# Shifted places for the stationary operands of gate and up, and a ring of eight places

## The chip, the cores and the metric

The kernel runs on one core of a Trainium2 chip. The metric is device time in microseconds (us), from the start to the end of one execution. Of the engines, TensorE (PE in the profile, its weight loads PEld) multiplies, VectorE (DVE), ScalarE (ACT) and GpSimd (POOL) do elementwise work, and SyncE's queue (SP) issues most DMAs.

## What is computed

The reference is one decoder layer. The change touches the first half of its last part, the products of a normalised activation with two weight matrices:

```python
fn = rms_norm(h, norm_ffn[l])                  # 1024 x 1024
g = fn @ ffn_w_gate[l]                         # 1024 x 2816
g_conv = ffn_conv_b[l] + sum(cw[i] * g_pad[:, i:i + s] for i in range(CONV_W))
h = h + (jax.nn.silu(g_conv) * (fn @ ffn_w_up[l])) @ ffn_w_down[l]
```

Ahead of it stand a gated linear attention, a causal attention, their output projection and a cross-attention over 256 memory tokens; none of them is touched.

## The kernel before, in words

All products keep float32 accuracy by splitting both operands into a high and a low part (`split`, L77: ScalarE writes the high part at L66, VectorE subtracts it and writes the low part at L69) and by multiplying three times: low by high, high by low, high by high.

Gate and up are computed in 11 pairs `j` of column blocks; a pair covers 256 columns of `ffn_w_gate` (`m_` 0, called g below) and the same of `ffn_w_up` (`m_` 1, called u). Each half is a 2 x 2 block product done with seven products in place of eight: P1, P6, P5, P7, P2, P3, P4, in this order (`ORDER`, L1328). Pairs 0 and 1 take P1 and P2 from matmuls made earlier, so that 146 products are left. Below, 2uP3 is product P3 of the up half of pair 2.

A product (`product`, L1214) is 12 matmuls, each with a 128 x 128 stationary operand from the weights and 512 moving columns from the activations (tiles `obP3` to `obP7`, `fh`, `fl`). They stand at L1220, L1221 and L1222.

The stationary operands of a product are made by `prep` (L1332). The raw weights of a half pair lie in a tile `rw` (1 MB, loaded by SyncE's queue in `raw_load`, L1231). For P1, P2 and P4 the source is a part of `rw`; for the others it is a sum in the tile `ss`, which GpSimd makes (VectorE for 0g). There is one `ss`, so the sums of a half pair start when the split of the P3 before it, the last reader, is done. The first three of the four GpSimd operations have to be over before P6 can be split. The split's result goes into a place `op`, 4096 bytes a partition: the high part, then the low part, each of four 128 x 128 blocks. Places are taken in turn from a list (`RING`). Seven are there at first; from 2uP1 on, two more join, whose room is held until then by the tiles `x1`. A place can be written again when TensorE has done the product that read it. `prep` runs 6 products ahead of `run` in pairs 0 and 1 and 8 ahead later (L1414).

After its products, `run` (L1368) adds PSUM banks into `GU` on VectorE. Two of these additions gate TensorE: P7 adds into the bank of P6, so it has to wait until `GU <- p, P` has read P6; P3 adds into the bank of P5, so it waits until `GU <- GU, P` has read P5. The tile `p` is ScalarE's copy of P1. Between them stand the convolution and silu of the gate (`conv`, two steps on VectorE at L72, two activations on ScalarE).

No order is written out by hand: a scheduler in the language's tile layer puts each engine's instructions into a queue by program order, priorities and its own costs, and each queue then runs strictly in that order.

Of the kernel before, what the change touches and what calls it, by code (L numbers as in the profile page):

```python
# [10 lines left out]
F32 = mybir.dt.float32  # L11
F32R = mybir.dt.float32r
# [6 lines left out]
P = 128  # L19
# [14 lines left out]
def build(tc, a, out):  # L34
# [6 lines left out]
    @contextmanager  # L41
    def pri(off):
        tc.cur_priority -= off
        yield
        tc.cur_priority += off
# [11 lines left out]
    def pool(name, side=None):  # L57
        return tc.tile_pool(name=name, bufs=1, reuse_waits="tile", **({"side": side} if side else {}))

    def k16(shape, dt, name):  # L60
        return big.tile(shape, dt, name=name, tag="k16", bufs=8)
# [3 lines left out]
    def act(o, i, f, **kw):  # L65
        nc.scalar.activation(out=o, in_=i, func=f, **kw)  # L66

    def tt(o, x, y, op, eng=None):
        (eng or nc.vector).tensor_tensor(out=o, in0=x, in1=y, op=op)  # L69
# [7 lines left out]
    def split(hi, lo, src, gain=None):  # L77
        if gain is None:
            act(hi, src, AF.Copy)
            tt(lo, src, f32(hi), ALU.subtract)  # L80
        else:
            act(hi, src, AF.Copy, scale=gain)
            stt(lo, src, gain, f32(hi), ALU.mult, ALU.subtract)
# [182 lines left out]
    def pj(n, name="pj"):  # L266
        pjn[0] += 1
        return pjc[pjn[0] % pjn[1]].tile([P, 512], F32, name=name, tag="pj", bufs=1)[:, 0:n]
# [11 lines left out]
    def proj(W, n, t):  # L280
        o = pj(n)
        mm3(o, [(xblk(xh, t)[:, k], xblk(xl, t)[:, k], W[k][0], W[k][1]) for k in range(KD)])
        return o
# [53 lines left out]
    for t in range(NB):  # L337
# [5 lines left out]
        o = proj(W, 256, t)  # L343
# [14 lines left out]
    for t in range(NB):  # L358
        o = proj(W, 304, t)
# [5 lines left out]
        x1, x2 = kpe[:, 0:16], kpe[:, 16:32]  # L365
# [34 lines left out]
    for mh in range(2):  # L400
        W = load_chunk((pBc, pAc)[mh], a["w_in"], C_Q + 256 * mh, 256, KD, f"wq{mh}", R_NM, wb=8)
        for m_ in range(2):
            for hf in range(2):
                o = pj(512)
# [292 lines left out]
    for u in us:  # L697
        for h in range(4):
            x = H()
# [529 lines left out]
    def raw_load(j, m):  # L1229
        RAW[j, m] = rwc[m].tile([P, KD, 2 * P], F32, name="rw", tag="rw", bufs=1)  # L1230
        nc.sync.dma_start(out=RAW[j, m], in_=a[("ffn_w_gate", "ffn_w_up")[m]][:, 2 * P * j:2 * P * (j + 1)].rearrange("(k p) n -> p k n", p=P))  # L1231
# [66 lines left out]
    for i in range(2):  # L1298
        fcc.tile([P, S], F32, name="conv", tag=f"conv{i}", bufs=1)
    RING = [(fcc, "op2"), (fcc, "op3"), (fcc, "op4")]  # L1300
    for pl, tg in RING:
        pl.tile([P, 2, 4, P], F32R, name="op", tag=tg, bufs=1)
    fsp = pool("fs"); fsc = fsp.__enter__()
    fsc.tile([P, 4, 4, P], F32, name="ss", tag="ss", bufs=1)
    rgp = pool("rg"); rgc = rgp.__enter__()
    for tg in ("op0", "op1"):
        rgc.tile([P, 2, 4, P], F32R, name="op", tag=tg, bufs=1)
    X1 = [rgc.tile([P, 2, 512], F32, name="x1", tag=f"op{i}", bufs=1) for i in (7, 8)]
    RING = [(rgc, "op0"), (rgc, "op1")] + RING + [(rgc, "op5"), (rgc, "op6")]
    rwp.append(pool("rw1", "right"))  # L1310
    rwc.append(rwp[1].__enter__())
    fps = psum("fps"); fpc = fps.__enter__()
# [4 lines left out]
    for i, nm in enumerate(("P1", "P2")):  # L1317
        for m_ in range(2):
            product(xb_[i][m_], WF[m_, 1][4 * i:4 * i + 4], nm, True)
            if i == 0:  # L1320
                act(X1[0][:, m_], xb_[0][m_], AF.Copy)
            else:
                tt(X1[1][:, m_], X1[0][:, m_], xb_[1][m_], ALU.add)
    GU = k16([P, 2, 2, S], F32, "GU")
# [4 lines left out]
    prods = [(j, m_, nm) for j in range(NP) for m_ in range(2) for nm in ORDER if j > 1 or nm not in ("P1", "P2")]  # L1329
    OPS, SS, BK, CV = {}, {}, {}, {}  # L1330

    def prep(j, m_, nm):  # L1332
        raw = RAW[j, m_]
        a11, a12, a21, a22 = raw[:, 0:4, 0:P], raw[:, 4:8, 0:P], raw[:, 0:4, P:], raw[:, 4:8, P:]
        ge = nc.vector if j == 0 and m_ == 0 else nc.gpsimd
        if nm == "P6":
            s_ = SS[j, m_] = fsc.tile([P, 4, 4, P], F32, name="ss", tag="ss", bufs=1)
            tt(s_[:, 0], a21, a22, ALU.add, ge)
            tt(s_[:, 1], s_[:, 0], a11, ALU.subtract, ge)
        if nm == "P7":  # L1340
            tt(SS[j, m_][:, 2], a11, a21, ALU.subtract, ge)
        if nm == "P3":
            tt(SS[j, m_][:, 3], a12, SS[j, m_][:, 1], ALU.subtract, ge)
        if nm in ("P1", "P2", "P4"):
            src = {"P1": a11, "P2": a12, "P4": a22}[nm]
        else:
            src = SS[j, m_][:, {"P5": 0, "P6": 1, "P7": 2, "P3": 3}[nm]]
        if (j, m_, nm) == (2, 1, "P1"):

            RING.extend([(rgc, "op7"), (rgc, "op8")])  # L1350
        pl, tg = RING.pop(0)
        RING.append((pl, tg))
        o = pl.tile([P, 2, 4, P], F32R, name="op", tag=tg, bufs=1)
        split(o[:, 0], o[:, 1], src)
        OPS[j, m_, nm] = [(o[:, 0, k], o[:, 1, k]) for k in range(4)]
        if nm == "P4" and j + 1 < NP:
            raw_load(j + 1, m_)
# [10 lines left out]
    def run(j, m_, nm):  # L1368
# [13 lines left out]
        if nm == "P6":  # L1382
            if j == 1:
                PA[m_] = X1[0][:, m_]
            tt(Y[:, 0, 512:], PA[m_], bk, ALU.add)
# [3 lines left out]
        if nm == ("P2" if j > 1 else "P7"):  # L1389
            c11 = X1[1][:, m_] if j == 1 else A2[0][:, m_]  # L1390
            if m_ == 0:
# [19 lines left out]

    done = 0
    for i, x in enumerate(prods):
        while done < min(len(prods), i + (6 if x[0] < 2 else 8)):  # L1414
            with pri(250 if done < 2 else 0):
                prep(*prods[done])
            done += 1
        run(*x)
# [35 lines left out]
    for i, (th, fs) in enumerate(steps):  # L1454
# [9 lines left out]
        for x, f in enumerate(fs):  # L1464
            for y, b in enumerate(BANKS):
                t, n = y // 2, y % 2
# [42 lines left out]
```

## Time and profile before

| | us |
|---|---|
| median of 2 runs | 1397.74 (1397.06 to 1398.41) |
| profiled execution, its own time | 1397.98 |
| its span, first to last instruction | 1396.3 |
| TensorE matmuls busy | 1361.8 (98%) |
| VectorE busy | 853.7 (61%) |
| ScalarE busy | 636.2 (46%) |
| GpSimd busy | 203.9 (15%) |

The span is what the trace covers; 1.7 us of the profiled execution lie around it. The products of gate and up run from 744.8 to 1152.4 us of the span. A matmul's busy time in the profile is longer than its distance to the next one, since matmuls are pipelined and their ends are modelled; the pace is read from their starts, or from a stretch divided by its count.

### The profile page before, as it was taken

To read this page: it belongs to the slowest core of one execution; us is meant where nothing else is said; L and a number is where in the kernel's file an instruction comes from. 1 tells how busy PE (TensorE), PEld (TensorE's weight loads), DVE (VectorE), ACT (ScalarE), POOL (GpSimd) and SP (SyncE) were. 2 spreads that over 40 slices of the span, in tenths; PEclk is the share of its full clock that TensorE was granted. 3 is DMA by queue.
4 is the path that set the end of the run, shared out by engine and by line. 5 is a ranking of instruction groups with operands and counts; after the bars stand their busy time and mean duration, and the time that the engine had idled before them with its cause. 6 is when DMAs were issued, how large, how long until landed. Compare 5 with 4: busy or idle time off the path is not lost.

```text
span 1396.3 us, 19231 instructions
## 1 busy us (share of the span) xinstructions
PE 1361.8 (98%) x7372; PEld 1135.5 (81%) x7372; DVE 853.7 (61%) x1628; ACT 636.2 (46%) x1312; POOL 203.9 (15%) x318
## 2 busy tenths in 40 slices
PE   8999999899999999999997999999999999999998
PEld 8977889788777787888875778888888888888887
DVE  6536785786686714577788776666666655325321
ACT  6424457777776703565544343333344344223220
POOL 0200001322231000000013333332233300000000
PEclk9999999999999999999998999999999999999999
DMA  6111010121002403201122222222222147346521
GB/s 216 45 53 31 9 38 20 40 67 35 1 1 77 137 0 106 76 16 46 61 76 90 92 91 91 91 75 77 91 91 91 46 143 264 131 170 229 180 106 61
DMA packets 71148, 117.16 MB, mean 84 GB/s; under 512 B 6537, under 2 KB 47632, under 8 KB 71056
## 3 DMA queue, kind: packets, MB, share of 16 engines
q1 hardware_dynamic: 70882, 115.87, 24.6%
q8 instruction: 58, 0.95, 0.3%
q14 instruction: 34, 0.28, 0.1%
q10 hardware_dynamic: 174, 0.06, 0.0%
HBM read 95.99 MB, written 19.92 MB: 83 GB/s over the span
## 4 chain that ended last, share of the span: by engine, by line
PE 85%; DVE 7%; issue 3%; ACT 3%; DMA 1%; POOL 0%; SPq 0%; ACTq 0%; DVEq 0%; POOLq 0%
PE pj L88 6%; PE pj L89 6%; PE pj L90 6%; PE dn L1470 6%; PE dn L1471 6%; PE dn L1469 6%; PE P L1220 6%; PE P L1221 5%; PE P L1222 5%; PE mo L756 3%; PE PTp L727 2%; PE A L1220 2%; PE A L1221 2%; PE A L1222 2%; PE S L88 2%
## 5 line engine op out<-in xcount | busy, mean ns | idle before, releaser
L1220 PE MATMUL P<-obP,op 128*128 128x512 f32 x352 | 139.2, 395 | 3.8 <-DVE GU L69 3.7
L1221 PE MATMUL P<-obP,op 128*128 128x512 f32 x352 | 138.2, 393 | 0.0
L1222 PE MATMUL P<-obP,op 128*128 128x512 f32 x352 | 138.0, 392 | 0.0
L1469 PE MATMUL dn<-wd,gt 128*128 128x512 f32 x352 | 136.9, 389 | 0.0
L1470 PE MATMUL dn<-wd,gt 128*128 128x512 f32 x352 | 136.9, 389 | 0.0
L1471 PE MATMUL dn<-wd,gt 128*128 128x512 f32 x352 | 136.9, 389 | 0.0
L69 DVE TENSOR_TENSOR wd<-rd,wd 128x1024 fp32r<-128x1024 f32 x44 | 52.8, 1223 | 94.6 <-ACT wd L66 94.6
L66 ACT ACTIVATE op<-ss 128x512 fp32r<-128x512 f32 x88 | 55.0, 629 | 112.8 <-PE P L1222 74.7
L69 POOL TENSOR_TENSOR ss<-rw 128x512 f32<-128x512 f32 x42 | 55.2, 1336 | 274.8 <-DVE op L69 243.8
L66 ACT ACTIVATE wd<-rd 128x1024 fp32r<-128x1024 f32 x44 | 45.6, 1056 | 97.8 <-PE dn L1471 50.1
L69 DVE TENSOR_TENSOR op<-rw,op 128x512 fp32r<-128x512 f32 x58 | 62.6, 1079 | 42.6 <-ACT op L66 42.5
L1220 PEld LDWEIGHTS P<-obP,op 128*128 128x128 f32 x352 | 66.8, 190 | 20.8 <-DVE GU L69 7.0
L1222 PEld LDWEIGHTS P<-obP,op 128*128 128x128 f32 x352 | 66.8, 190 | 14.2
L1221 PEld LDWEIGHTS P<-obP,op 128*128 128x128 f32 x352 | 66.9, 190 | 13.7
L1469 PEld LDWEIGHTS dn<-wd,gt 128*128 128x128 f32 x352 | 66.1, 188 | 13.8
L1471 PEld LDWEIGHTS dn<-wd,gt 128*128 128x128 f32 x352 | 66.1, 188 | 13.6
L1470 PEld LDWEIGHTS dn<-wd,gt 128*128 128x128 f32 x352 | 66.1, 188 | 13.6
L66 ACT ACTIVATE op<-rw 128x512 fp32r<-128x512 f32 x58 | 36.5, 631 | 84.7 <-PE P L1222 64.4
L69 DVE TENSOR_TENSOR op<-ss,op 128x512 fp32r<-128x512 f32 x88 | 62.8, 721 | 13.8 <-ACT op L66 13.0
L72 DVE SCALAR_TENSOR_TENSOR conv<-GU,cols,conv 128x1023 f32<-128x1023 f32 (+1 forms) x44 | 56.9, 1298 | 3.7 <-ACT conv L66 3.3
L717 DVE TENSOR_REDUCE mx<-S 128x1 f32<-128x128 f32 (+7 forms) x64 | 48.1, 752 | 15.5 <-PE S L715 15.2
L1220 PE MATMUL A<-fh,op 128*128 128x512 f32 x144 | 56.0, 389 | 0.0
(421 smaller groups left out, 3626.9 us busy)
## 6 DMA issues: line engine op xcount, KB each, us to landing
rd<-in_ffn_w_down SPq DMA_DIRECT2D x44, 512.0 KB
rw<-in_ffn_w_gate SPq DMA_DIRECT2D x11, 1024.0 KB
rw<-in_ffn_w_up SPq DMA_DIRECT2D x11, 1024.0 KB
gdr<-conv SPq DMA_DIRECT2D x22, 512.0 KB
rgd<-gdr SPq DMA_DIRECT2D x44, 256.0 KB
mraw<-in_xa_w_kv SPq DMA_DIRECT2D x16, 256.0 KB
hh<-in_x SPq DMA_DIRECT2D x2, 2048.0 KB
raw_wo<-in_w_out SPq DMA_DIRECT2D x8, 512.0 KB
```

Source lines behind the costliest of these rows:

```text
L66: nc.scalar.activation(out=o, in_=i, func=f, **kw)
L69: (eng or nc.vector).tensor_tensor(out=o, in0=x, in1=y, op=op)
L72: nc.vector.scalar_tensor_tensor(out=o, in0=x, scalar=s, in1=y, op0=op0, op1=op1)
L88: mm(o, lhsT=ll, rhs=rh, start=i == 0, stop=False)
L89: mm(o, lhsT=lh, rhs=rl, start=False, stop=False)
L90: mm(o, lhsT=lh, rhs=rh, start=False, stop=last and i == n - 1)
L1220: mm(o, lhsT=wl, rhs=bh[:, k], start=start and k == 0, stop=False, **kw)
L1221: mm(o, lhsT=wh, rhs=bl[:, k], start=False, stop=False, **kw)
L1222: mm(o, lhsT=wh, rhs=bh[:, k], start=False, stop=k == 3, **kw)
L1469: mm(ob[b], lhsT=gl, rhs=wh, start=f == 0, stop=False)
L1470: mm(ob[b], lhsT=gh, rhs=wl, start=False, stop=False)
L1471: mm(ob[b], lhsT=gh, rhs=wh, start=False, stop=f == NF - 1)
```

## The change

Every place of the ring grows from 1024 to 1152 float32 elements a partition (4096 to 4608 bytes), and there are eight instead of nine, so that the room is the same 36864 bytes. An operand starts 64 bytes times the place's number into its place, and 32 bytes further for pairs of odd number: sixteen starts that lie 32 bytes apart, from 0 to 480. The first six places are there from the start, the last two join at 2uP1, and `x1` lies in those two until then. `prep` runs 5 products ahead in pairs 0 and 1 and 7 ahead later. No instruction is added or removed, and none changes its size.

```diff
     RING = [(fcc, "op2"), (fcc, "op3"), (fcc, "op4")]
     for pl, tg in RING:
-        pl.tile([P, 2, 4, P], F32R, name="op", tag=tg, bufs=1)
+        pl.tile([P, 9 * P], F32R, name="op", tag=tg, bufs=1)
...
     for tg in ("op0", "op1"):
-        rgc.tile([P, 2, 4, P], F32R, name="op", tag=tg, bufs=1)
-    X1 = [rgc.tile([P, 2, 512], F32, name="x1", tag=f"op{i}", bufs=1) for i in (7, 8)]
-    RING = [(rgc, "op0"), (rgc, "op1")] + RING + [(rgc, "op5"), (rgc, "op6")]
+        rgc.tile([P, 9 * P], F32R, name="op", tag=tg, bufs=1)
+    X1 = [rgc.tile([P, 9 * P], F32, name="x1", tag=f"op{i}", bufs=1)[:, 0:8 * P].rearrange("p (m n) -> p m n", m=2) for i in (6, 7)]
+    RING = [(rgc, "op0"), (rgc, "op1")] + RING + [(rgc, "op5")]
...
         if (j, m_, nm) == (2, 1, "P1"):
-            RING.extend([(rgc, "op7"), (rgc, "op8")])
+            RING.extend([(rgc, "op6"), (rgc, "op7")])
         pl, tg = RING.pop(0)
         RING.append((pl, tg))
-        o = pl.tile([P, 2, 4, P], F32R, name="op", tag=tg, bufs=1)
+        sh = 16 * int(tg[2]) + 8 * (j % 2)
+        o = pl.tile([P, 9 * P], F32R, name="op", tag=tg, bufs=1)[:, sh:sh + 8 * P].rearrange("p (q k n) -> p q k n", q=2, k=4)
         split(o[:, 0], o[:, 1], src)
...
-        while done < min(len(prods), i + (6 if x[0] < 2 else 8)):
+        while done < min(len(prods), i + (5 if x[0] < 2 else 7)):
```

The scheduler orders the queues anew. From pair 4 on, each engine has the same kinds of work in the same rhythm, and TensorE's products follow each other one by one as before. In pairs 0 to 3 the queues differ; three places follow.

**Place one, ScalarE in pair 0.** Before; `op_8499`, `op_8516`, `op_8482`, `op_8535` and `op_8556` are the high parts of 0uP5, 0uP7, 0uP6, 0uP3 and 0uP4, `op_8600` and `op_8583` those of 1gP5 and 1gP6; `conv_8575` is the convolution of the second block of the pair, `conv_8551` that of the first:

```order
L66 ACTIVATE op_8499<-ss_8479 128x512
L66 ACTIVATE op_8516<-ss_8479 128x512
L66 ACTIVATE op_8482<-ss_8479 128x512
L66 ACTIVATE op_8535<-ss_8479 128x512
L66 ACTIVATE op_8556<-rw_8398 128x512
L66 ACTIVATE op_8600<-ss_8580 128x512
L66 ACTIVATE conv_8575<-GU_8456,cols_80 128x1024
L66 ACTIVATE op_8583<-ss_8580 128x512
L66 ACTIVATE conv_8551<-GU_8456,cols_80 128x1024
```

After; 0uP5, 0uP6, 0uP7, 0uP3 are `op_8512`, `op_8496`, `op_8531`, `op_8553`, then 1gP6 is `op_8597`, 0uP4 is `op_8575`, and the convolutions are `conv_8570` and `conv_8547`:

```order
L66 ACTIVATE op_8512<-ss_8493 128x512
L66 ACTIVATE op_8496<-ss_8493 128x512
L66 ACTIVATE op_8531<-ss_8493 128x512
L66 ACTIVATE op_8553<-ss_8493 128x512
L66 ACTIVATE op_8597<-ss_8594 128x512
L66 ACTIVATE conv_8570<-GU_8456,cols_80 128x1024
L66 ACTIVATE op_8575<-rw_8398 128x512
L66 ACTIVATE conv_8547<-GU_8456,cols_80 128x1024
```

The split of 1gP6 has moved ahead of the first convolution, and that of 0uP4 behind it.

**Place two, VectorE in pair 0.** Before, from the addition that follows 0gP7:

```order
L69 TENSOR_TENSOR GU_8456<-p1_8262,P6_8485 128x512
L69 TENSOR_TENSOR op_8556<-rw_8398,op_8556 128x512
L69 TENSOR_TENSOR GU_8456<-GU_8456,P5_8502 128x512
L69 TENSOR_TENSOR GU_8456<-GU_8456,D2_8561 128x512
L69 TENSOR_TENSOR op_8600<-ss_8580,op_8600 128x512
L72 SCALAR_TENSOR_TENSOR conv_8575<-GU_8456,cols_80,conv_8575 128x1023
```

After, from the same addition to the one that P6 of the up half needs before 0uP7:

```order
L69 TENSOR_TENSOR GU_8456<-p1_8262,P6_8479 128x512
L69 TENSOR_TENSOR op_8553<-ss_8493,op_8553 128x512
L69 TENSOR_TENSOR GU_8456<-GU_8456,P5_8499 128x512
L69 TENSOR_TENSOR GU_8456<-GU_8456,D2_8556 128x512
L69 TENSOR_TENSOR op_8597<-ss_8594,op_8597 128x512
L72 SCALAR_TENSOR_TENSOR conv_8570<-GU_8456,cols_80,conv_8570 128x1023
L69 TENSOR_TENSOR GU_8456<-GU_8456,P5_8499 128x512
L72 SCALAR_TENSOR_TENSOR conv_8570<-GU_8456,cols_80,conv_8570 128x1022
L69 TENSOR_TENSOR op_8575<-rw_8398,op_8575 128x512
L72 SCALAR_TENSOR_TENSOR conv_8547<-GU_8456,cols_80,conv_8547 128x1023
L69 TENSOR_TENSOR GU_8456<-p1_8276,P6_8580 128x512
```

The low part of 0uP4 has moved from the second row to behind both convolution steps, and that of 0uP3 stands where it stood. On TensorE the first three matmuls of 0uP4 now stand between 0uP5 and 0uP7, and the other nine and one of 1gP6 between 0uP7 and 0uP3; before, ten matmuls of 0uP4 stood between 0uP7 and 0uP3.

**Place three, ScalarE in pair 2.** Before; `op_8964` and `op_8985` are 2uP3 and 2uP4, `op_9029` is 3gP6, and `p1_9024` is the copy of 2uP1:

```order
L66 ACTIVATE op_8964<-ss_8893 128x512
L66 ACTIVATE conv_8980<-GU_8456,cols_80 128x1024
L66 ACTIVATE op_8985<-rw_8754 128x512
L66 ACTIVATE op_9029<-ss_9026 128x512
L66 ACTIVATE conv_9004<-GU_8456,cols_80 128x1024
L66 ACTIVATE conv_8980<-conv_8980 128x1024
L66 ACTIVATE p1_9024<-A2_8878 128x512
```

After; 2uP3 is `op_8982`, 3gP6 is `op_9043`, and the copy of 2uP1 is `p1_9021`:

```order
L66 ACTIVATE conv_8976<-GU_8456,cols_80 128x1024
L66 ACTIVATE op_8982<-ss_8907 128x512
L66 ACTIVATE conv_8976<-conv_8976 128x1024
L66 ACTIVATE conv_8999<-GU_8456,cols_80 128x1024
L66 ACTIVATE p1_9021<-A2_8875 128x512
L66 ACTIVATE op_9043<-ss_9040 128x512
```

The split of 3gP6, which stood three instructions ahead of the copy of 2uP1, now stands behind it; 2uP4 has gone further up the queue, into one of the two new places.

## Rows read from the trace of the kernel before

**Rows 1.** Page, busy time, share and instructions of each engine
```profile
PE 1361.8 (98%) x7372; PEld 1135.5 (81%) x7372; DVE 853.7 (61%) x1628; ACT 636.2 (46%) x1312; POOL 203.9 (15%) x318
```
**Rows 2.** Stretch: length; PE, PEld, DVE, ACT, POOL busy us (x); PEclk; DMA share; GB/s
```profile
900.00:1140.00 240.00, 240.00 (x1060) 198.72 (x1059) 159.44 (x194) 93.76 (x132) 64.52 (x47) 1.00 0.24 80
```
**Rows 3.** Matmuls of places, 740 to 1156 us: duration min/median/max, first and last start
```profile
L1220 PE MATMUL D<-obP,op x88: 388/389/795, 744.8 to 1151.8; 128*128 128x512 f32 x88
...
L1222 PE MATMUL D<-obP,op x88: 389/389/628, 746.1 to 1152.2; 128*128 128x512 f32 x88
```
**Rows 4.** Waits of TensorE, 750 to 1152 us: us in total, times, longest
```profile
PE P L1220 <- DVE GU L69: 3.7, 4, 2.0
```
**Rows 5.** TensorE in order of time: start us, us, what, [idle before <-releaser]
```profile
759.96 0.50 PE L1220 MATMUL P<-obP,op 128*128 128x512 f32 x1 [0.53 <-DVE GU L69]
...
773.99 0.50 PE L1220 MATMUL P<-obP,op 128*128 128x512 f32 x1 [0.90 <-DVE GU L69]
...
788.21 0.50 PE L1220 MATMUL P<-obP,op 128*128 128x512 f32 x1 [0.28 <-DVE GU L69]
...
813.52 0.50 PE L1220 MATMUL P<-obP,op 128*128 128x512 f32 x1
```
**Rows 6.** TensorE in order of time, 832 to 840 us
```profile
832.48 0.39 PE L1222 MATMUL P<-obP,op 128*128 128x512 f32 x1
834.83 0.50 PE L1220 MATMUL P<-obP,op 128*128 128x512 f32 x1 [1.96 <-DVE GU L69]
...
836.42 0.63 PE L1222 MATMUL P<-obP,op 128*128 128x512 f32 x1
...
838.55 0.63 PE L1221 MATMUL P<-obP,op 128*128 128x512 f32 x1
...
839.28 0.40 PE L1220 MATMUL A<-fh,op 128*128 128x512 f32 x1
```
**Rows 7.** Weight loads by line, 840 to 1140 us: count, busy us, mean ns
```profile
L1221 PEld LDWEIGHTS P<-obP,op 128*128 128x128 f32 x251 | 47.1, 188 | 9.7
```
**Rows 8.** VectorE by line, 840 to 1140 us: count, busy us, mean ns
```profile
L69 DVE TENSOR_TENSOR op<-ss,op 128x512 fp32r<-128x512 f32 x61 | 42.1, 690 | 11.3 <-ACT op L66 10.6
L72 DVE SCALAR_TENSOR_TENSOR conv<-GU,cols,conv 128x1023 f32<-128x1023 f32 (+1 forms) x32 | 40.8, 1276 | 1.8 <-ACT conv L66 1.4
```
**Rows 9.** VectorE in order of time, 757 to 761 us and at 834 us
```profile
757.21 0.69 DVE L69 TENSOR_TENSOR GU<-p,P 128x512 f32<-128x512 f32 x1 [1.07 <-PE P L1222]
757.87 1.44 DVE L69 TENSOR_TENSOR op<-rw,op 128x512 fp32r<-128x512 f32 x1
759.23 0.67 DVE L69 TENSOR_TENSOR GU<-GU,P 128x512 f32<-128x512 f32 x1
...
834.10 0.68 DVE L69 TENSOR_TENSOR GU<-p,P 128x512 f32<-128x512 f32 x1
```
**Rows 10.** ScalarE in order of time, 829 to 833 us
```profile
829.29 0.64 ACT L66 ACTIVATE op<-ss 128x512 fp32r<-128x512 f32 x1 [3.92 <-POOL ss L69]
829.83 1.23 ACT L66 ACTIVATE conv<-GU,cols 128x1024 f32<-128x1024 f32 x1
830.97 1.04 ACT L66 ACTIVATE conv<-conv 128x1024 f32<-128x1024 f32 x1
831.92 0.58 ACT L66 ACTIVATE p<-A 128x512 f32<-128x512 f32 x1
```
**Rows 11.** GpSimd and ScalarE in order of time, 756 to 762 us
```profile
756.21 2.55 POOL L69 TENSOR_TENSOR ss<-rw 128x512 f32<-128x512 f32 x2 [1.83 <-DVE op L69]
758.72 1.73 POOL L69 TENSOR_TENSOR ss<-ss,rw 128x512 f32<-128x512 f32 x1
...
760.73 1.25 ACT L66 ACTIVATE conv<-GU,cols 128x1024 f32<-128x1024 f32 x1 [1.25 <-DVE GU L69]
```
**Rows 12.** SyncE's issue of pair 3's gate load, and ScalarE waiting for it
```profile
805.00 0.38 SPq L1231 DMA_DIRECT2D rw<-in_ffn_w_gate  x1
...
810.57 0.63 ACT L66 ACTIVATE op<-rw 128x512 fp32r<-128x512 f32 x1 [1.32 <-DMA rw<-in_ffn_w_gate]
```

## The prediction

> **What bounds the kernel now.** I read the page's busy times first: TensorE is busy for 98% of the span [rows 1], so what counts is its pace and its waits. The pace comes from a stretch of gate and up without any wait: 1060 matmuls in 240.00 us, 0.2264 us each, at full granted clock, the higher of the two levels, 2.4 GHz [rows 2]. At that pace a product of 12 takes 2.72 us and the 146 products, 1752 matmuls, 396.7 us. They take 407.6 us in the trace (first start 744.8, last start 1152.2 and 0.2 for that matmul) [rows 3], so some 11 us are lost, all of it before 840 us or at the very end.
>
> The waits of TensorE tell where. From 750 us on it waits four times for an addition of VectorE, 3.7 us in all, the longest 2.0 us [rows 4]. Three lie in pairs 0 and 1 [rows 5], the longest in pair 2 [rows 6]. In each, the addition that reads a PSUM bank is late, not the operand of the product.
>
> **What the shift does to the pace.** The edit moves where stationary operands start. It adds no instruction, so it can act through the weight load, through the matmul, or through the two splits that write the operands.
>
> A weight load takes 188 ns [rows 7] of a matmul's 226, beside the matmul before it. It could grow by 38 ns before TensorE noticed. The splits run 17 us or more ahead of their product once the ring is full (eight places of 2.72 us are 21.8, less the product that is read and the split itself), and VectorE is busy for 159.44 of 240 us [rows 2]: even if a split's 690 ns [rows 8] doubled, one more in every 2.72 us would fit.
>
> For the matmul, the trace bounds the effect on one side. While the granted clock is at its lower level, 1.2 GHz, five matmuls take 2.13 us (836.42 to 838.55) [rows 6], 426 ns each: 512 columns at that clock are 426.7, with nothing left over. At the higher level 512 columns are 213.3, and the pace is 226.4. So 13.1 ns a matmul are something other than columns. If all of it came from reads of the two operands that meet in the memory, and the shift parted them, 1752 times 13.1 ns would be 23.0 us. No row of before has a stationary operand of this size off the 512-byte grid (places of 4096 bytes, blocks of 512), so the trace can't tell. I take 0: the 13.1 ns are the same in every one of these matmuls whichever tiles it reads, which looks like a fixed cost of changing the operand, not like meetings that come and go. The bounds stay: 23.0 us down, and up whatever a load beyond 226 ns costs.
>
> The Trainium skill gives another figure for the pace: "TensorE: Matmul & The Clock Gate", section "Back-to-back issue gap", has N / 2.4 + 2.5 ns for an isolated gap of a warm matmul, 215.8 ns for 512 columns. The row's 226.4 disagrees. By the page's figure 1752 times 10.6 ns, an estimate of 18.6 us, would be there to win, and the sum below would come out at 1377.1.
>
> **What the smaller ring does where it is full.** From pair 4 on a split starts when a place comes free. With one place less it starts one product later, 2.72 us, out of some 20 us of lead; the additions keep their place in each queue relative to TensorE's products. No wait is seen there now, and I price this at 0.
>
> **What the new order does, place by place.** This is where the sum comes from.
>
> *Pair 2, the longest wait.* TensorE started 2uP5's last matmul at 832.48 and 2uP7's first at 834.83 [rows 6]. The addition it waited for ran at 834.10 on VectorE [rows 9]. It needs the copy of 2uP1, which ScalarE made only at 831.92: ahead of it in the queue stood the split of 3gP6, which had kept ScalarE idle for 3.92 us until GpSimd's sums were there at 829.29, and two activations of the convolution [rows 10]. Then the clock fell: 2uP7 took from 834.83 to 839.28 [rows 6], 4.45 us instead of 2.72. The cost is 834.83 - 832.48 - 0.23 = 2.12, and 1.73 for clock and restart, 3.85 us together. After, the copy stands ahead of 3gP6 (place three). What it then waits for is the convolution of 2g: 2uP3's split begins when 2gP4 is done, three products before the end of 2uP5, about 824.5; its two halves (0.63, 0.69) and a convolution step of 1.28 to 1.8 beside GpSimd's sums put the end of VectorE's second step near 827.8, ScalarE's two activations (1.04 and 1.23) near 830.1 and the copy near 830.7; behind one more step of 1.28 the addition is over near 832.6, and TensorE comes for it at 832.7. The wait goes: -3.85. If it doesn't, 0.
>
> *Pairs 1 and 2, two small ones.* 1gP3 starts at 788.21 after 0.28 us of idling [rows 5], with restart 0.45 late; 2gP7, at 813.52 [rows 5], is 0.28 late with its restart. Before the first stood the split of 1uP4, which is replaced by the shorter one of 1uP3; the second addition now stands ahead of the two splits that held it. Both go: -0.7.
>
> *Pair 0, where the order gets worse.* Now 0gP3 starts at 759.96, 0.53 idle [rows 5], since 0uP4's split of 1.44 us stands ahead of the addition on VectorE [rows 9]. After, 0uP3's split stands there (place two). With six places it can only begin when 0gP7 is done, at 757.2; at 690 ns it ends near 758.6 and the addition near 759.3, just in time: 0.65 gained, and TensorE comes to the end of 0uP5 at 766.8. But GpSimd's sums for pair 1 can start only behind that split, at 758.6 rather than 756.21, and what P6 needs is there 4.24 us later (756.21 to 760.45) [rows 11], near 762.9. ScalarE's split of 1gP6 now waits for it ahead of the first convolution (place one), which then begins near 763.5 rather than at 760.73 [rows 11]. On VectorE follow step, addition, step (1.28, 0.67, 1.28 [rows 8, 9]) and 0uP4's split: ready near 768.5, where TensorE wants it at 766.8, 1.7 late. Behind it one more step and the addition that 0uP7 needs: near 770.5, 1.1 late. 0uP3, which started at 773.99 [rows 5] with three matmuls fewer done (0.68), starts near 776.2. So 776.2 - 773.99 - 0.68 = 1.5 us lost. The two new waits, 2.8 us within 4, are as long as the one after which the clock fell in pair 2; if it falls here too, 1.73 more. I take about half of that, 0.9: +2.4. The bounds are -1.5 (all waits of pair 0 gone) and +3.3.
>
> **The sum.** 1397.98 (the profiled execution; the median of the runs is 0.24 lower) - 3.85 - 0.7 + 2.4 + 0 for pace and ring = **1395.8**.
>
> **The rivals.** *A, slower: a split at the head of ScalarE's queue takes the place of the wait removed.* 3gP1, now in a new place, stands on ScalarE between 2uP6 and 2uP5, and it needs pair 3's gate load. That took from 805.00 to 810.57 [rows 12], 5.6 us from issue to use. The load is issued when 2gP4 is split, which after is near 810.1 rather than 804.9, so it lands near 815.8. The addition that 2gP3 needs stands behind 2uP5's split: near 818.9, against 819.05 when TensorE comes. [...] With 2.5 us late, 1.73 for the clock and pair 0 at its upper bound: 1397.98 - 4.55 + 3.3 + 4.2 = 1400.9. For it: the margin is 0.15 us. Against: this stretch has little other traffic. It decides from 2.3 us of lateness, where a wait of 2.2 us has used up the forecast's gain.
>
> *B, the shift parts reads that met.* Up to 23.0 us, 1372.8. For it: those 13.1 ns vanish at the lower clock, as a shortage of reads would. Against: they are alike in all matmuls. The Trainium skill's page "SBUF — State Buffer", section "Who interferes with whom", gives TensorE two read ports that don't depend on each other; by it nothing is to be won here, and no run so far shows it.
>
> *C, a shifted operand is read more slowly.* Only a load longer by over 38 ns would show; each 10 ns beyond would cost 17.5 us, 1413.3. Nothing in the profile speaks for it but that no row has tried it.
>
> **How the numbers follow.** The forecast has 0.64 (1392 to 1399, its own range), A 0.20 (1399 to 1404), B 0.08, C 0.08. A range from 1390 to 1403 leaves out most of B and C and the tail of A, some 0.17. About 2% is what a measurement of this kernel can tell from no change, 28 us: B falls just short of it, so faster by over 2% has 0.02, slower, from C alone, 0.02, and the rest is within 2%.
>
> **What would show it.** In the profile after: the pace from 900 to 1140 us should still be 240.00 us for 1060 matmuls; a smaller or larger count there is B or C, and it would differ between places or pairs. The wait near 832 us should be gone, and ScalarE's copy of 2uP1 should stand before 831 us. Near 767 to 770 us two waits of 1 to 2 us should stand, for a split of 0uP4 and an addition. A wait of 2gP3 near 819 us behind a load on ScalarE would be A. I am wrong if waits appear from pair 4 on, since then the ring's lead was needed, or if TensorE's matmuls of even and odd pairs differ.

## The result and the profile after

The changed kernel takes 1408.84 us (median of 2 runs, 1408.82 to 1408.85) against 1397.74 before: 1.0079 times as long, 95% interval 1.0055 to 1.0104. Forecast were 1395.8, with a range of 1390 to 1403. The change costs 11 us.

The page's busy times, which answer [rows 1], say little: TensorE is still busy nearly all the time, only longer.

```profile
PE 1371.6 (97%) x7372; PEld 1134.1 (81%) x7372; DVE 867.4 (62%) x1628; ACT 636.6 (45%) x1312; POOL 212.6 (15%) x318
```

The stretch from 900 to 1140 us, which answers [rows 2], says where the time went (columns as there):

```profile
900.00:1140.00 240.00, 239.92 (x1030) 192.66 (x1029) 166.65 (x190) 90.10 (x129) 73.70 (x48) 1.00 0.22 75
```

1030 matmuls in place of 1060, at the same full clock (2.4 GHz) and with TensorE busy throughout: each takes some 6 ns longer. A stretch's count also takes in matmuls that reach over its ends, so the pace is better read from starts: in pairs 3 to 9, waits left out, they lie 226.7 ns apart before and 232.5 after. GpSimd and VectorE are also busier than in [rows 2], by 9.2 and 7.2 us, with about as many instructions. Weight loads are recorded at 188 ns, as in [rows 7] (from 900 to 1140 us; line, engine, operation, shapes, count | busy, mean ns | idle before):

```profile
L1220 PEld LDWEIGHTS P<-obP,op 128*128 128x128 f32 x196 | 36.8, 188 | 10.8 <-DVE GU L69 2.3
```

TensorE's waits from 750 to 1163 us (us in total, times, longest), which answer [rows 4], and the matmuls behind the three longest of them:

```profile
PE P L1220 <- DVE GU L69: 2.4, 3, 1.4
PE D L1220 <- DVE op L69: 0.9, 1, 0.9
```

```profile
769.88 0.50 PE L1220 MATMUL D<-obP,op 128*128 128x512 f32 x1 [0.93 <-DVE op L69]
...
771.67 0.50 PE L1220 MATMUL P<-obP,op 128*128 128x512 f32 x1 [0.83 <-DVE GU L69]
...
824.12 0.50 PE L1220 MATMUL P<-obP,op 128*128 128x512 f32 x1 [1.44 <-DVE GU L69]
```

The first two are 0uP4 and 0uP7, in the places that the forecast gave; the wait of 2uP7 at 832 us [rows 6] is gone. The third is 2gP3, rival A. From the starts of products in the traces, in us:

| stretch | before | after |
|---|---|---|
| 0gP4 to 3gP1 (pairs 0 to 2) | 102.66 | 103.06 |
| 3gP1 to 10gP1 (pairs 3 to 9) | 266.56 | 274.92 |
| 10gP1 to the last matmul of gate and up | 38.22 | 38.87 |

That is 9.4 of the 10.8 us by which the span grew; the other 1.4 lie ahead of gate and up, where nothing was changed and where profiled executions of unchanged stages differ by as much (gate and up began between 744.55 and 746.44 us in the kernels below).

Which matmuls are slower can be read from the first matmuls of products in order of time. 6gP1 starts at 967.17 with a stationary operand that lies 256 bytes off a multiple of 512, 6gP6 at 969.89 (320), 6gP5 at 972.69 (0), 6gP7 at 975.44 (64):

```profile
967.17 0.39 PE L1220 MATMUL A<-fh,op 128*128 128x512 f32 x1
...
969.89 0.40 PE L1220 MATMUL P<-obP,op 128*128 128x512 f32 x1
...
972.69 0.39 PE L1220 MATMUL P<-obP,op 128*128 128x512 f32 x1
...
975.44 0.40 PE L1220 MATMUL P<-obP,op 128*128 128x512 f32 x1
```

6gP1 takes 2.72 us, the old pace; 6gP6 takes 2.80; 6gP5 takes 2.75. Over all products from 756 us on, the mean distance from a matmul's start to the next, by where its stationary operand starts (modulo 512, without distances over 250 ns), is:

| start, bytes | 0 | 32 | 64 | 96 | 128 | 160 | 192 | 224 | 256 |
|---|---|---|---|---|---|---|---|---|---|
| ns a matmul | 229.6 | 233.4 | 233.2 | 234.1 | 232.3 | 233.2 | 230.8 | 233.3 | 227.5 |

From 288 to 480 the figures repeat those from 32 to 224 within 0.4 ns. Only multiples of 256 come near the old 226.7, and after some matmuls reach it. By the addresses in the built programs all moving operands of gate and up lie at multiples of 512, as all stationary ones did before.

### The profile page after: what moved, and what is told of

Read it like the earlier page. It is cut to its first block, busy times and chain, and to the rows that moved or that the text cites. A ratio compares the mean times of both kernels' runs of the same rounds, so it can differ in the third digit from the quotient of the medians.

```text
span 1407.1 us, 19242 instructions
## 1 busy us (share of the span) xinstructions
PE 1371.6 (97%) x7372; PEld 1134.1 (81%) x7372; DVE 867.4 (62%) x1628; ACT 636.6 (45%) x1312; POOL 212.6 (15%) x318
## 4 chain that ended last, share of the span: by engine, by line
PE 82%; DVE 8%; issue 3%; ACT 3%; DMA 2%; POOL 1%; SPq 0%; ACTq 0%; DVEq 0%; POOLq 0%
PE dn L1470 6%; PE dn L1472 6%; PE dn L1471 6%; PE pj L88 6%; PE pj L89 5%; PE pj L90 5%; PE P L1220 5%; PE P L1221 5%; PE P L1222 5%; PE mo L756 3%; PE PTp L727 2%; PE A L1222 2%; PE A L1220 2%; PE A L1221 2%; PE S L88 2%
## 5 line engine op out<-in xcount | busy, mean ns | idle before, releaser
L1220 PE MATMUL P<-obP,op 128*128 128x512 f32 x352 | 141.1, 401 | 2.6 <-DVE GU L69 2.4
L1221 PE MATMUL P<-obP,op 128*128 128x512 f32 x352 | 139.6, 397 | 0.0
L1222 PE MATMUL P<-obP,op 128*128 128x512 f32 x352 | 139.4, 396 | 0.0
L72 DVE SCALAR_TENSOR_TENSOR conv<-GU,cols,conv 128x1023 f32<-128x1023 f32 (+1 forms) x44 | 67.9, 1548 | 3.5 <-ACT conv L66 3.1
L1222 PE MATMUL A<-fh,op 128*128 128x512 f32 x144 | 56.8, 394 | 0.0
L1220 PE MATMUL A<-fh,op 128*128 128x512 f32 x144 | 56.7, 394 | 0.0
```

What stands on the lines that cost most here:

```text
L72: nc.vector.scalar_tensor_tensor(out=o, in0=x, scalar=s, in1=y, op0=op0, op1=op1)
L1220: mm(o, lhsT=wl, rhs=bh[:, k], start=start and k == 0, stop=False, **kw)
L1221: mm(o, lhsT=wh, rhs=bl[:, k], start=False, stop=False, **kw)
L1222: mm(o, lhsT=wh, rhs=bh[:, k], start=False, stop=k == 3, **kw)
```

## The experiments

Three theories were tried first. *Grid*: a stationary operand off a multiple of 256 bytes slows its matmuls. *Variety*: operands that start differently from one another do. *Ring*: the smaller ring and its order cost the time, the shift none.

**The ring alone, and a shift on the grid.** Both with the ring of eight and the order of after:

```diff
-        sh = 16 * int(tg[2]) + 8 * (j % 2)
+        sh = 0                        # the ring alone
+        sh = 64 * (int(tg[2]) % 2)    # multiples of 256 bytes
```

> The ring of eight places of 4608 bytes, with the shift set to 0; the order of the instructions is that of after. Grid theory (a stationary operand whose start is not a multiple of 256 bytes makes each of its matmuls some 6 ns longer; the ring has no part in it): the pace goes back to 1060 matmuls in 240 us, and the time is that of after less 1752 x 6.6 ns, 11.6 us: 1397.2, within 1.5 of it; the waits of after stay (2gP3 1.6 us near 822, 0uP4 and 0uP7 about 1 us each). Ring theory (fewer places and the new order slow TensorE, the shift doesn't): 1030 in 240 us as in after, 1408.8.

> Ring of eight; places of odd number start 256 bytes in, places of even number at 0, so that starts still change from product to product. Grid theory: multiples of 256 cost nothing, 1060 in 240 us, 1397.2. Variety theory (operands that start differently from place to place are what slows TensorE, wherever they start): slower than the run without shift, 1040 or fewer in 240 us, over 1402.

Measured: 1403.62 us (the ring alone), 1.0034 times before (1.0021 to 1.0047), and 1403.17 (multiples of 256), 1.0035 (1.0022 to 1.0048). None of the theories had this: the ring costs 5 us and the shift another 6. The stretches of both, the waits of the ring alone from 850 to 1140 us, and one of them:

```profile
900.00:1140.00 240.00, 238.26 (x1045) 195.34 (x1045) 169.75 (x193) 91.82 (x132) 73.60 (x48) 1.00 0.23 79
900.00:1140.00 240.00, 238.26 (x1045) 195.30 (x1044) 168.59 (x193) 90.57 (x131) 73.59 (x48) 1.00 0.23 78
```

```profile
PE P L1220 <- DVE GU L69: 2.0, 7, 0.3
```

```profile
1028.72 0.39 PE L1222 MATMUL P<-obP,op 128*128 128x512 f32 x1
1029.40 0.50 PE L1220 MATMUL P<-obP,op 128*128 128x512 f32 x1 [0.29 <-DVE GU L69]
1029.74 0.40 PE L1221 MATMUL P<-obP,op 128*128 128x512 f32 x1
```

The pace between waits is the old one, 226.8 ns, but in each of pairs 3 to 9 P7 of the up half waits: 0.68 us from the matmul ahead to its first and 0.34 to the next, where 0.23 each is the pace, so 0.56 a pair and 3.9 us for seven. From 3gP1 to 10gP1 it takes 270.68 us, 4.1 over before. Variety is out: with starts that alternate on the grid the pace is that without a shift.

**All places shifted alike**, by 128 (`sh = 32`) and by 32 bytes (`sh = 8`):

> Ring of eight; every place starts 128 bytes in, none differs from another. Grid theory: all matmuls are off the grid, about 232.3 ns each as those at 128 in after, so about 1033 in 240 us and 1397.2 + 1752 x 5.9 ns = 1407.5. Variety theory: as without shift, 1397.2. Line theory (only starts off multiples of 64 bytes cost, since a row then touches one more line of 64): as without shift, 1397.2.

> Ring of eight; every place starts 32 bytes in. Grid theory: 233.4 ns a matmul as those at 32 in after, about 1028 in 240 us, 1397.2 + 1752 x 7 ns = 1409.5. Line theory: slower too, 1409 or more, and clearly slower than the run with all places 128 bytes in. Variety theory: 1397.2.

Measured: 1408.75 us, 1.0074 (1.0057 to 1.009), and 1409.54, 1.008 (1.0065 to 1.0095), with

```profile
900.00:1140.00 240.00, 240.00 (x1028) 192.85 (x1027) 165.93 (x190) 89.93 (x129) 73.68 (x48) 1.00 0.22 75
```

```profile
900.00:1140.00 240.00, 240.00 (x1026) 192.00 (x1025) 165.28 (x189) 89.51 (x128) 73.64 (x48) 1.00 0.22 75
```

So far the grid theory holds, and the variety and line theories fall: one shift for all is as dear as sixteen, and 128 bytes, a multiple of 64, cost nearly as much as 32. A matmul between waits is 5.7 ns (128) and 6.5 ns (32) longer in pairs 3 to 9, 10 and 11.4 us for 1752 of them; over the ring alone the times rise by only 5 to 6, because a slower TensorE meets VectorE's additions later: by the starts the seven waits cost 1.5 us (128) and 1.2 us (32) in place of 3.9, and those of pairs 0 to 2 cost 0.9 and 1.6 us less. Each of the two costs hides part of the other.

**Why the ring makes P7 wait.** VectorE and GpSimd in the ring alone, pair 7, from the split behind the addition that follows 7gP3 (columns: start, us, engine, what; TensorE's 7uP7 then waits until 1029.40):

```profile
1018.93 1.63 DVE L69 TENSOR_TENSOR op<-rw,op 128x512 fp32r<-128x512 f32 x1
1020.48 2.31 DVE L72 SCALAR_TENSOR_TENSOR conv<-GU,cols,conv 128x1023 f32<-128x1023 f32 x1
1022.72 0.68 DVE L69 TENSOR_TENSOR GU<-GU,D 128x512 f32<-128x512 f32 x1
1023.32 1.72 DVE L72 SCALAR_TENSOR_TENSOR conv<-GU,cols,conv 128x1022 f32<-128x1022 f32 x1
...
1028.67 0.68 DVE L69 TENSOR_TENSOR GU<-p,P 128x512 f32<-128x512 f32 x1
```

```profile
1017.47 2.55 POOL L69 TENSOR_TENSOR ss<-rw 128x512 f32<-128x512 f32 x2 [13.53 <-DVE op L69]
1019.96 1.75 POOL L69 TENSOR_TENSOR ss<-ss,rw 128x512 f32<-128x512 f32 x1
1021.79 2.16 POOL L69 TENSOR_TENSOR ss<-rw,ss 128x512 f32<-128x512 f32 x1
```

and the same place in the kernel before:

```profile
1016.95 1.55 DVE L69 TENSOR_TENSOR op<-rw,op 128x512 fp32r<-128x512 f32 x1
1018.42 1.27 DVE L72 SCALAR_TENSOR_TENSOR conv<-GU,cols,conv 128x1023 f32<-128x1023 f32 x1
...
1025.12 0.68 DVE L69 TENSOR_TENSOR GU<-p,P 128x512 f32<-128x512 f32 x1
```

```profile
1013.58 1.31 POOL L69 TENSOR_TENSOR ss<-rw 128x512 f32<-128x512 f32 x1
1014.82 1.75 POOL L69 TENSOR_TENSOR ss<-ss,rw 128x512 f32<-128x512 f32 x1
1016.66 1.30 POOL L69 TENSOR_TENSOR ss<-rw,ss 128x512 f32<-128x512 f32 x1
```

With one place less the split of P3 (here 7uP3) comes one product later, and GpSimd's sums for the next half pair, which wait for it, too. Before, they were over at 1017.96, ahead of the convolution; now they lie beside it, and its two steps take 2.31 and 1.72 us in place of 1.27. VectorE has no gap there, so the addition that P7 waits for is late by that 1.5 us. GpSimd slows as well (2.16 for 1.30). An addition that reads a PSUM bank keeps its 0.68 us beside the sums. This is what the Trainium skill's page "SBUF — State Buffer", section "Who interferes with whom", states: a VectorE instruction with two inputs in SBUF contends with a GpSimd instruction that reads SBUF, one with at most one SBUF input (outside modes that use two ports) doesn't. The trace agrees: the steps have two SBUF inputs, the addition has one.

To test it, the sums were left out from pair 3 on, in the ring alone, with the same order of work on TensorE, ScalarE and VectorE:

```diff
-        if nm == "P6":
+        if nm == "P6" and j < 3:
...
-        if nm in ("P1", "P2", "P4"):
-            src = {"P1": a11, "P2": a12, "P4": a22}[nm]
+        if j > 2 or nm in ("P1", "P2", "P4"):
+            src = {"P1": a11, "P2": a12, "P4": a22}.get(nm, a21)
```

> Ring of eight, no shift, and from pair 3 on GpSimd's sums are left out: P6, P5, P7 and P3 split a part of the raw weights instead (that part of the computation is left out). The order on VectorE and ScalarE is that of the ring of eight without shift. Sums theory (with one place less the sums start one product later and lie beside the convolution steps on VectorE, which take 2.31 and 1.72 us instead of 1.27; the addition that P7 of the up half waits for is late by that): the steps take 1.27 each, the seven waits of 0.29 idle and about 0.57 in all near 874, 912.7, 951 ... 1106 us are gone, 1060 matmuls in 240 us, and the time is 4 us below the ring of eight without shift: 1399 to 1400. Lead theory (a split starts one product later, and the addition stands behind it on VectorE; the sums have no part): the seven waits stay, 1045 in 240 us, 1403.5.

Measured: 1397.9 us, 0.9997 of before (0.9988 to 1.0007); the seven waits are gone, and the steps take 1.28 and 1.27:

```profile
900.00:1140.00 240.00, 240.00 (x1061) 198.72 (x1059) 147.06 (x195) 93.92 (x132) 0.00 (x0) 1.00 0.23 76
```

```profile
1017.58 1.28 DVE L72 SCALAR_TENSOR_TENSOR conv<-GU,cols,conv 128x1023 f32<-128x1023 f32 x1 [0.69 <-ACT conv L66]
...
1019.38 1.27 DVE L72 SCALAR_TENSOR_TENSOR conv<-GU,cols,conv 128x1022 f32<-128x1022 f32 x1
```

The lead theory is out: the splits are as late as in the ring alone (7uP3's low part starts 1.35 us behind 7gP3's first matmul in both), and nothing waits. The time lies 1 to 2 us below what was expected. In the profiled executions pairs 0 to 2 account for 1.7 us: when gate and up began, only four matmuls lay some 0.43 us apart (1.2 GHz) here and ten in the ring alone, 1.2 us, and pair 2 is 0.4 us shorter without the sums of 3g.

**Where a stationary operand lies, or how far from the moving one?** First the kernel before with everything on the left, stationary and moving, 128 bytes further:

```diff
-    padr.tile([P, 120], F32, name="padr", tag="padr", bufs=1)
+    padr.tile([P, 88], F32, name="padr", tag="padr", bufs=1)
+    padl = es.enter_context(tc.tile_pool(name="padl", bufs=1))
+    padl.tile([P, 32], F32, name="padl", tag="padl", bufs=1)
```

then the ring of eight with the same padding and `sh = 32`, which puts the stationary operands back on a multiple of 256 while the moving ones stay 128 off.

> The kernel before (nine places, its own order) with 128 bytes of padding moved from the right end of the memory to the left, so that all tiles on the left lie 128 bytes further: stationary and moving operands of gate and up both start at 128 off a multiple of 256, and so do those of the output product after them. Grid theory (what counts is where the stationary operand itself starts): about 232.3 ns a matmul, 1033 in 240 us, and gate and up some 10 us longer, the down stage (1056 matmuls) 6 us longer too: 1410 or more. Relative theory (what counts is where the stationary operand lies against the moving one): as before, 1060 in 240 us, 1398.

> Ring of eight; everything on the left lies 128 bytes further, so that the moving operands of gate and up start at 128 off a multiple of 256, and the shift of 128 in each place puts the stationary operands back on a multiple of 256. Own theory (a stationary operand on a multiple of 256 is quick, wherever the moving one lies): 1045 in 240 us as the ring of eight without shift, 1403.2. Relative theory (only the distance between the two starts counts): about 232.3 ns a matmul, 1028 in 240 us as with all places 128 bytes in, 1408.8. The down stage, where both lie at 128, keeps its pace by the relative theory.

Measured: 1398.25 us, 1.0 (0.9991 to 1.0009), and 1409.93, 1.0076 (1.0062 to 1.009). The stretches of gate and up, and of the down stage, of the first and then of the second:

```profile
900.00:1140.00 240.00, 240.00 (x1060) 198.75 (x1059) 158.53 (x193) 93.58 (x133) 65.71 (x48) 1.00 0.24 79
1165.00:1390.00 225.00, 225.00 (x994) 186.32 (x993) 72.35 (x83) 57.63 (x72) 0.00 (x0) 1.00 0.43 150
```

```profile
900.00:1140.00 240.00, 240.00 (x1029) 193.05 (x1028) 166.68 (x190) 88.81 (x128) 73.68 (x48) 1.00 0.22 75
1165.00:1390.00 225.00, 225.00 (x994) 186.29 (x993) 81.48 (x93) 62.97 (x79) 0.00 (x0) 1.00 0.48 167
```

The grid theory falls, the relative one holds, from both sides: off the grid together costs nothing, in gate and up or in the down stage (994 in 225 us is 226.4 ns); on the grid against a moving operand that is off it costs as much as the reverse.

**One part shifted, and small steps.** In the first the high part starts 128 bytes in and the low part on a multiple of 256 (`hi = t_[:, 32:32 + 4 * P]`, `lo = t_[:, 5 * P:9 * P]`); in the second `sh = int(tg[2])`, 4 bytes a place.

> Ring of eight; only the high part starts 128 bytes in, the low part on a multiple of 256. Of the three matmuls of a block the first loads the low part, the other two the high part. If each load pays for itself: two of three matmuls at about 232, one at 226.5: 230.4 in the mean, 1042 less the waits, about 1037 in 240 us, 1405. If one load off the grid disturbs its neighbours as well: about 232 for all three, 1030, 1408.

> Ring of eight; places start 0, 4, 8 ... 28 bytes in, by their number. If the distance counts in blocks (all starts within the same 32 or 64 bytes are alike): all at 226.7 as without shift, 1045 in 240 us, 1403. If any distance other than a multiple of 256 costs: 233 for seven of eight places, 1030, 1408. If some small distance parts the two streams of reads and is quicker: matmuls of that place below 226.

Measured, one run each and so without an interval: 1409.5 us with 1026 matmuls in the stretch, and 1408.45 with 1032:

```profile
900.00:1140.00 240.00, 240.00 (x1026) 191.95 (x1026) 165.79 (x189) 89.93 (x129) 73.62 (x48) 1.00 0.22 75
```

```profile
900.00:1140.00 240.00, 239.78 (x1032) 192.95 (x1031) 167.05 (x190) 90.08 (x129) 73.71 (x48) 1.00 0.22 75
```

With only the high part off, a matmul starts 233.8 ns behind the one ahead of it where it loads the high part, and 232.2 where it loads the low part, which is on the grid; counted to the next start the figures are 232.6 and 234.8. Either way both are slow: one load off disturbs its neighbours. With small steps the means, counted from the start ahead, are 232.6, 230.3, 231.3, 232.0, 232.8, 230.1 and 233.5 ns for 4, 8, 12 ... 28 bytes; at 0, from pair 3 on, the first three matmuls of a product take 232, 231 and 227, the rest 226.3 to 227.1. So already 4 bytes cost, and no distance tried was quicker than none.

The trace of before shows where this stops. In an early stage, from 41 to 68 us, 192 float32r matmuls of 304 moving columns have their stationary operand, three and three in turn, at 0 and at 64 bytes from the moving one (modulo 256, by the built program). They take 139.4 and 138.3 ns. Matmuls of 256 columns at distance 0 take 120 ns (median) in the same trace, 13.3 more than their columns at 2.4 GHz; 304 columns and 13.3 ns would be 140.0. So at 304 columns, with 64 bytes on every second three, no cost shows; other distances weren't tried there.

**The wait in pair 2, and a quicker kernel.** All three have before's nine places without shift. The first lets the last two places join at 3gP1, with a look-ahead of 7 from pair 2 on; the second lets them join at 2gP1; the third is the first with the sums of 3g made by VectorE:

```diff
-        if (j, m_, nm) == (2, 1, "P1"):
+        if (j, m_, nm) == (3, 0, "P1"):    # in the second: (2, 0, "P1")
...
-        while done < min(len(prods), i + (6 if x[0] < 2 else 8)):
+        while done < min(len(prods), i + (6 if x[0] < 2 else 7)):    # in the second as before
...
-        ge = nc.vector if j == 0 and m_ == 0 else nc.gpsimd
+        ge = nc.vector if (j, m_) in ((0, 0), (3, 0)) else nc.gpsimd    # the third alone
```

> The kernel before, nine places without shift; the last two places join at 3gP1 instead of 2uP1, and the look-ahead from pair 2 on is 7 instead of 8. On ScalarE the copy of 2uP1 then stands ahead of 3gP1 and 3gP6, on VectorE both second steps and the low part of 3gP1 ahead of the addition. If the wait near 832 is ScalarE's wait for 3gP6's sums alone: it goes with its clock fall, 3.85 us, pairs 3 to 10 stay without waits, 1394.3 against 1398.2. If the smaller ring through pair 2 only moves a wait to pair 3 (sums of 3u beside the convolution steps): one or two waits of about 0.6 there, 1395.5; if 3gP1's place comes too late: no gain.

> The kernel before, nine places without shift; the last two places join at 2gP1, one half pair earlier than before. The split of 2uP3 then starts two places earlier, so that 3g's sums on GpSimd start earlier and lie beside less of the convolution. If the wait near 832 comes from GpSimd's sums lying beside the convolution of 2g (steps of 1.7 and 1.8 instead of 1.27, and the split of 3gP6 late for the sums): the steps of 2g take 1.27, the wait and its clock fall go, 3.85 us, and pair 2 looks like pairs 3 to 9 of before: 1394.5 against 1398.4. If 2uP1 and 2uP6 now stand on ScalarE or VectorE ahead of work that 2g's products wait for (their places are free only when x1 has been read): a wait of 1 us or more between 805 and 822 in place of it, 1396 to 1399.

> The kernel before, nine places without shift, with the last two places joining at 3gP1 and a look-ahead of 7 from pair 2 on, and the four sums of 3g made by VectorE instead of GpSimd. With the join alone the copy of 2uP1 was in time (over at 830.5), but VectorE ran eight instructions beside GpSimd's sums (steps of 1.8, 1.72 and 3.63 for two, a split of 1.78) and the addition came at 834.63, 1.8 us late. Sums theory: without GpSimd beside them the steps take 1.27 and the split 0.69, which is 3.5 us less, and the four sums cost VectorE about 0.63 each, of which three lie ahead of the addition: it is over near 832.9 to 833.3, against 832.8 wanted; the wait shrinks from 1.8 to 0.5 or less and the clock doesn't fall: 1395 to 1396 against 1398.5. Lead theory (the addition is late since its own inputs are, whoever makes the sums): the wait near 833 stays at 1.8 or grows, 1397.4 or more.

Measured: 1397.36 us, 0.9989 (0.998 to 0.9998); 1398.32, 0.9993 (0.9984 to 1.0002); 1394.98, 0.997 (0.9958 to 0.9982). The first came out above both gains expected: the copy of 2uP1 is over at 830.49, and still 2uP7 waits 1.77 us until 835.37, since VectorE works beside the sums, of which the third ends at 831.72 (the convolution's second pair of steps, 1.28 each when alone, a split and the addition):

```profile
830.48 3.63 DVE L72 SCALAR_TENSOR_TENSOR conv<-GU,cols,conv 128x1023 f32<-128x1023 f32 x2
834.03 0.69 DVE L69 TENSOR_TENSOR op<-rw,op 128x512 fp32r<-128x512 f32 x1
834.63 0.68 DVE L69 TENSOR_TENSOR GU<-p,P 128x512 f32<-128x512 f32 x1
```

In the second that wait goes, and one of 2.58 us stands ahead of 2gP7 (817.12): a split that waits for 2u's sums is now ahead of its addition.

```profile
815.27 1.20 DVE L69 TENSOR_TENSOR op<-ss,op 128x512 fp32r<-128x512 f32 x1 [1.84 <-ACT op L66]
816.39 0.67 DVE L69 TENSOR_TENSOR GU<-p,P 128x512 f32<-128x512 f32 x1
```

In the third no wait is left in pair 2; from 2gP1 to 3gP1 it takes 40.9 us against 44.6 in the first and 45.05 before. That is the quickest kernel of the study.

```profile
829.82 1.28 DVE L72 SCALAR_TENSOR_TENSOR conv<-GU,cols,conv 128x1023 f32<-128x1023 f32 x1
831.01 0.68 DVE L69 TENSOR_TENSOR ss<-ss,rw 128x512 f32<-128x512 f32 x1
831.62 1.28 DVE L72 SCALAR_TENSOR_TENSOR conv<-GU,cols,conv 128x1022 f32<-128x1022 f32 x1
832.81 0.68 DVE L69 TENSOR_TENSOR op<-rw,op 128x512 fp32r<-128x512 f32 x1
833.41 0.68 DVE L69 TENSOR_TENSOR GU<-p,P 128x512 f32<-128x512 f32 x1
```

## Why the prediction was wrong

**The pace, taken as 0: this step failed most.** It measured 5.8 ns a matmul in pairs 3 to 9 (274.92 - 266.56 us, less 1.54 of waits, over 1176 matmuls), and 9.2 us over all of gate and up, where matmuls behind a wait had been slow before too. (The pace in the sum, 226.4, came from a count; by starts it is 226.7, which makes 13.1 ns 13.3 and changes nothing else.) The argument was that 13.1 ns are the same in every matmul and so no meeting of reads. That spoke against a gain, and the loss was left to one mechanism, a load over 38 ns longer (rival C). C's direction was right and its mechanism not: loads are still recorded at 188 ns, and the distance between the two operands' starts decides. The bound above, "whatever a load beyond 226 ns costs", was no bound, since it named one way only. Rival B didn't come: no distance tried was quicker than 226 ns. The Trainium skill's page "SBUF — State Buffer", section "Who interferes with whom", named with B, gives the two reads independent ports; the two runs with the padding (226.4 and 233 ns) show a pace that depends on how the two operands lie to one another, so by that rule the loss couldn't be seen coming. The 215.8 ns that the prediction takes from the Trainium skill's page "TensorE: Matmul & The Clock Gate", section "Back-to-back issue gap", were not reached at any distance tried.

**The ring where it is full, priced at 0: failed.** The step looked at the lead of the splits, which is ample, and at the order of the additions, which is kept. It overlooked GpSimd's sums, which move with the split of P3 and land beside the convolution: 3.9 us in the ring alone. In the changed kernel 1.54 of them are left, since TensorE is slower. That the sums slow VectorE was at hand: the steps take 1.28 us in the mean of [rows 8], and the prediction itself wrote 1.8 for one beside the sums, in pair 2 alone.

**Pair 2, -3.85, and rival A (0.20).** The wait near 832 went, as forecast. But its cause was only half the copy of 2uP1: with the copy in time the sums beside VectorE still held the addition. In the changed kernel the waits ahead, 2gP3's above all, also let TensorE come later. Rival A came true by the path described: the load of 3's gate is issued at 816.04 and used at 821.50, and 2gP3's addition stands behind 2uP5's split.

```profile
821.50 0.64 ACT L66 ACTIVATE op<-rw 128x512 fp32r<-128x512 f32 x1 [4.20 <-DMA rw<-in_ffn_w_gate]
```

```profile
822.78 0.69 DVE L69 TENSOR_TENSOR op<-ss,op 128x512 fp32r<-128x512 f32 x1
823.38 0.68 DVE L69 TENSOR_TENSOR GU<-GU,P 128x512 f32<-128x512 f32 x1
```

The estimate of landing, 815.8, was 5.7 early because the issue was put at 810.1 and came at 816.04; the time from issue to use, 5.5 us, was right. The step that failed is the end of 2gP4's split, after which the load is issued. Its high part starts on ScalarE at 811.05, its low part on VectorE only at 815.30. VectorE has no gap from 807.72 on, and GpSimd makes the sums of 2u beside it from 807.88 to 814.83:

```profile
809.65 2.32 DVE L69 TENSOR_TENSOR conv<-conv,GU 128x1024 f32<-128x1024 f32 x1
...
812.49 1.19 DVE L69 TENSOR_TENSOR op<-rw,op 128x512 fp32r<-128x512 f32 x1
813.60 1.78 DVE L69 TENSOR_TENSOR conv<-conv,GU 128x512 f32<-128x512 f32 x1
815.30 0.68 DVE L69 TENSOR_TENSOR op<-rw,op 128x512 fp32r<-128x512 f32 x1
```

The first three take 1.22, 0.69 and 0.68 us where no sums lie beside them, 2.7 us less together. So the overlap that makes P7 wait seems to be behind this wait too; no run leaves out the sums of 2u, so it is not shown. With a margin of 0.15 us A deserved more than 0.20. The 1.73 us of lower clock that A's sum adds didn't come: the granted clock stayed at 2.4 GHz behind the wait of 1.44 us here. In the ring alone pair 2 is 1.2 us shorter than before (43.87 against 45.05), not 3.85.

**Pairs 0 and 1, +2.4 and -0.45: size off.** Both waits of pair 0 came where they were forecast, 1.1 and 1.0 us long (forecast 1.7 and 1.1), and no lower clock followed, neither here nor in the ring alone. That was luck: behind the same two waits seven or eight matmuls of 0uP7 lay 0.43 us apart in four of the eight other kernels with this order (multiples of 256, the high part alone, the moving operand by 128, steps of 4), so a price of half of 1.73 was fair. New small waits of P7 in pair 1 were not foreseen. From 0gP4 to 2gP1 the ring alone takes 58.68 us against 57.61, +1.1 where +1.95 was forecast.

Pairs 0 to 2 together come out 0.1 us shorter in the ring alone, forecast -2.15. In the changed kernel the waits and slow matmuls of these pairs (distances of starts over 250 ns, less 226.7 each) sum to 1.35 us less than before, since the slower TensorE meets the additions later. So the 13.0 us between forecast and result are the pace (9.2), the waits of pairs 3 to 9 (1.5), these 0.8, and the 1.4 by which the stages ahead of gate and up took longer in this execution.

## What to carry to other kernels

When an edit moves addresses under float32r matmuls of 512 columns, keep the distance between the starts of the two operands a multiple of 256 bytes: here every other distance tried cost 3 to 7 ns on each of 1752 matmuls. For other widths try it, since at 304 columns 64 bytes showed no loss. When a buffer is taken away, follow not only the work that waits for it but also what is released by that work: here GpSimd's sums, which moved beside VectorE's two-input steps. A bound from above must not rest on a single mechanism, and two costs of which one slows the waiting engine hide each other, so try them apart.

## What the runs showed of the hardware that was not expected

- Distances of 4 to 224 bytes between stationary and moving operand (mod 256) take 230 to 234 ns a matmul of 512 columns instead of 226.7, with the weight load recorded at 188 ns as before. How the two reads meet stays open: no run shows the mechanism. It was read for matmuls of 512 columns in float32r; at 304 columns a distance of 64 bytes showed no cost (138.3 against 139.4 ns).
- The slower pace carries over: after an operand off the grid the first three matmuls on it still take 227 to 232 ns with steps of 4, and the first six up to 236 in 6gP5 of the changed kernel; with one of two parts off, the other is slow as well.
- The lower clock doesn't follow the length of a wait alone: after a wait of 0.82 us near 770 in the kernel with alternating starts (multiples of 256) eight matmuls lay some 0.43 us apart (1.2 GHz); in the changed kernel none did after 0.83 us in the same place, nor after 1.44 at 824.
